# Attention of a hybrid decoder layer: a written order on four engines in place of a scheduled one, and row minima in place of row maxima

## The chip, the core and the metric

One core of a Trainium2 chip runs the whole layer in one launch. The metric is the device time of that launch in microseconds (us). The engines named below work side by side, each through its own queue in order: TensorE (PE, with its weight loads shown as PEld), VectorE (DVE), ScalarE (ACT), GpSimd (POOL) and SyncE (SP), which issues the transfers from memory. One waits for another only where a semaphore makes it.

## What is computed

A decoder layer on 512 positions of width 1024, in float32: RMS norm, one input projection, eight attention heads of 64 beside a gated linear recurrence, an output projection, then a gated feed-forward part. The change touches the attention heads alone. With 512 positions in blocks of 256 and three blocks to choose, every earlier block is chosen, so the attention is plain causal attention with a bias by distance:

```python
scale = HEAD_DIM ** -0.5
...
s_own = jnp.einsum("bhqd,bhkd->bhqk", qc, k_own) * scale
s_own = s_own + bias_T[head, t5_bucket(q_pos - k_pos)]
s_own = jnp.where(q_pos >= k_pos, s_own, -jnp.inf)
...
p = jax.nn.softmax(logits, axis=-1)
out = jnp.einsum("bhqk,bhkd->bhqd", p, v)
...
mix = jnp.concatenate([attn, lru], axis=-1) @ w_out
```

## The kernel before

Products are made from split operands. A float32 tile is cast to an upper half by ACT (`split`, line 84) and the rest, the lower half, is made by DVE (line 85); a product is then three matmuls (`mm3`, lines 79 to 81). Weights are split the same way: one 128x1024 cast on ACT (`wh`) and one subtraction of the same size on DVE (`wl`).

Attention goes by pairs of heads (`pr`, four of them, 128 rows of q and k each), in a pair by heads (`s`, two) and in a head by blocks of 128 queries (`i`, four). A tile (`pr`, `s`, `i`) covers the 128(i+1) keys up to its queries. Its steps, with the names that the trace uses:

- `psc`, two matmuls (lines 636 and 637): scores, first with the upper half of the keys (`sk`), then with the lower half (`klz`);
- `st`: line 640 on DVE adds the bias (`tb`) and takes the row's maximum, line 643 scales that maximum by a constant, line 644 on ACT takes the exponential and its sum, lines 646 and 647 on DVE take the reciprocal and scale the row;
- `ptp`, one transpose for each block of 128 keys (line 653), split into `pTh` (ACT) and `pTl` (DVE);
- after a head's last tile `pav`, eight matmuls with the values (line 663), drained by ACT and DVE into `pair` (lines 666, 667). After a pair's second head `pair` is split into `mixT`, the left operand of the output projection.

A pair's q and k come from `pq`: 16 pieces of three matmuls each, 48 matmuls in all; `pq` is then cast and subtracted into `sq`, `sk` and `klz` (lines 623 to 627). There is one `klz` tile for all pairs. PSUM banks are three for `pq` (shared later with `py`), two for `psc`, two for `ptp` and one for `pav`.

Up to line 578 the order on PE, ACT, DVE and SP is the order in which the code is written (`manual_schedule`, closed by `written.close()`). From there on a scheduler decides, by its own model of the engines, which ready instruction each queue gets next. The code of the attention only gives it a first order: `softmax` of a tile comes three tiles (`LAG`) ahead of its transposes, and three pieces (`FILL`) of the next pair's projection follow each tile. The scheduler fills PE with matmuls of the output projection (`py`) once the projections `pq` are used up.

Of the kernel before, what the change touches and what calls it, by code (L numbers as in the profile page):

```python
# [18 lines left out]
P = 128  # L19
S = 512  # L20
# [19 lines left out]
ISCALE = DH ** -0.5  # L40
FE = S + P
EW = 3 * P
FILL = 3
LAG = 3
assert MAX_DISTANCE <= P

# [6 lines left out]
def hybrid_layer(  # L53
# [16 lines left out]
    def bank(name, tag):  # L70
        return ps.tile([P, 512], F32, tag=tag, name=name, bufs=BANKS[tag])
# [26 lines left out]
    def at(hl, *idx):  # L98
        return hl[0][idx], hl[1][idx]
# [469 lines left out]
    for t in range(NT):  # L569
        pg = bank("pgr", "mm")  # L570
        for k in range(KD):
            mm3(pg, at(w_gr[t], slice(None), k), at(hT, slice(None), k), k == 0, k == KD - 1)
        if t >= 2:
            first_w.append(split_w(first_qk[:, :, t - 2], KD, P))
# [17 lines left out]
    heads = {}  # L592
# [5 lines left out]
    def head_pair(pr):  # L598

        tb = ap_.tile([P, 2, S], F32, tag="tb", name="tb")  # L600
# [6 lines left out]
        if pr:  # L607
            raw = load_qk(pr)
        ws = [split_w(raw[:, :, i], KD, P) for i in range(2)] if pr else first_w
        yield  # L610

        proj = []
        for w in ws:
            pq = bank("pq", "mm")
            for k in range(KD):
                mm3(pq, at(w, slice(None), k), at(hT, slice(None), k), k == 0, k == KD - 1)
                yield
            proj.append(pq)
        qs, ks = (ap_.tile([P, 2, S], F32R, tag=f"s{i}", name=f"s{i}") for i in "qk")
        kl = klz  # L620
        for s in range(2):
            me, other = own[s], own[1 - s]
            nc.scalar.copy(qs[me, s], proj[0][me])
            nc.vector.tensor_sub(qs[other, s], proj[0][me], f32(qs[me, s]))
            nc.scalar.copy(ks[me, s], proj[1][me])
            nc.scalar.copy(ks[other, s], proj[1][me])
            nc.vector.tensor_sub(kl[me, s], proj[1][me], f32(ks[me, s]))
        heads[pr] = qs, ks, kl, tb

    def softmax(pr, s, i):  # L630

        qs, ks, kl, tb = heads[pr]
        W = P * (i + 1)
        psc = bank("psc", "sc")
        qi = slice(i * P, (i + 1) * P)
        nc.tensor.matmul(psc[:, :W], qs[:, s, qi], ks[:, s, :W], start=True, stop=False)
        nc.tensor.matmul(psc[:, :W], qs[:, s, qi], kl[:, s, :W], start=False, stop=True)
        st = ap_.tile([P, S], F32, tag="st", name="st", bufs=4)
        sm = ap_.tile([P, 4], F32, tag="sm", name="sm", bufs=4)
# [7 lines left out]
        nc.vector.tensor_scalar(st[:, :W], st[:, :W], sm[:, 3:4], None, op0=ALU.mult)  # L647
        return st

    def transposed(st, pT, i):  # L650
        ptr = bank("ptp", "tr")
        for j in range(i + 1):
            nc.tensor.transpose(ptr[:, j * P:(j + 1) * P], st[:, j * P:(j + 1) * P], ident)  # L653
        split(by_keys(pT[0], i), by_keys(pT[1], i),
              ptr[:, :P * (i + 1)].rearrange("p (j q) -> p j q", q=P))

    def attend(pr, s, pT, pair):
        me, other = own[s], own[1 - s]
        pav = bank("pav", "av")
        for j in range(NT):  # L660
            vs = vhl[:, j, pr, 2 * s:2 * s + 2].rearrange("p a d -> p (a d)")
            for i in range(2):
                nc.tensor.matmul(  # L663
                    pav[:, j * P:], vs, pT[i][:, j * S:j * (S - P) + S],
                    start=j == 0 and i == 0, stop=j == NT - 1 and i == 1)
        nc.scalar.copy(pair[me], pav[other])
        nc.vector.tensor_add(pair[me], pav[me], pair[me])
        if s == 1:
            split(mixT[0][:, pr], mixT[1][:, pr], pair)

    tiles = [(pr, s, i) for pr in range(NPAIR) for s in range(2) for i in range(NT)]
    for _ in head_pair(0):
        pass
    ahead, sts, last = iter(()), [], None
    for n in range(-LAG, len(tiles)):
        if 0 <= n + LAG < len(tiles):
            pr, s, i = tiles[n + LAG]
            if s == 0 and i == 0:  # L680
                for _ in ahead:
                    pass
                if pr + 1 < NPAIR:
                    ahead = head_pair(pr + 1)
                    next(ahead)
            sts.append(softmax(pr, s, i))
        for _ in itertools.islice(ahead, FILL):
            pass
        if n < 0:
            continue  # L690
        pr, s, i = tiles[n]
        if i == 0:
            if last:
                attend(*last)
            if s == 0:
                pair = ap_.tile([P, S], F32, tag="pair", name="pair", bufs=1)
            pT = [ap_.tile([P, 3 * (S - P) + S], F32R, tag=f"pT{j}", name=f"pT{j}", bufs=1)
                  for j in "hl"]
            last = pr, s, pT, pair
        transposed(sts.pop(0), pT, i)  # L700
    attend(*last)

    attn_stack.close()

# [194 lines left out]
```

## Time and profile before

| | us |
|---|---|
| median of 3 runs | 585.26 (585.23 to 585.57) |
| the profiled execution | 586.3 |
| its span, first to last instruction | 584.2 |
| PE busy | 572.6 (98%) |
| PE weight loads busy | 473.5 (81%) |
| DVE busy | 360.3 (62%) |
| ACT busy | 279.7 (48%) |
| mean granted TensorE clock | 0.997 of full speed |

The profiled execution stands 2.1 us above its span and 1.0 us above the median of the timed runs. Shares of busy time are means over stages with different limits. A matmul's duration is longer than its distance to the next one, since matmuls are pipelined: its cost is read from one start to the next. The same holds for DVE and ACT, whose instructions overlap a little.

### The profile page before, as it was taken

The numbers are of one execution on the slowest core, as the hardware profiler recorded it, in microseconds if no ns is written. First come the engines' busy times: TensorE is split into PE (matmuls) and PEld (weight loads), VectorE is DVE, ScalarE is ACT, GpSimd is POOL, SyncE is SP. The second block draws the span as 40 slices with busy tenths as digits, with TensorE's granted clock in tenths as the row PEclk, the third lists the DMA queues.
The fourth block names the chain that finished last, engine by engine and source line by source line (L and its number), as shares of the span: only waits on it lengthen the run. The fifth ranks groups of instructions, "written<-read, shape, count | busy, mean of one in ns | idle before, by whom it ended". The sixth has DMA issues, their size and how long they took to land.

```text
span 584.2 us, 7051 instructions
## 1 busy us (share of the span) xinstructions
PE 572.6 (98%) x2734; PEld 473.5 (81%) x2734; DVE 360.3 (62%) x649; ACT 279.7 (48%) x457; POOL 15.9 (3%) x37
## 2 busy tenths in 40 slices
PE   8999999999999999999999999999999999999995
PEld 4988888787788889888888888888888888888884
DVE  5787777889896895656656656656656522241225
ACT  6568856778775663543444444344344322132121
POOL 2150000000000000000000000000000000000000
PEclk9999999999999999999999999999999999999998
DMA  9533626333202614012412422422424223332103
GB/s 269 157 109 115 212 72 193 98 107 108 73 1 70 217 44 139 1 55 90 145 63 82 144 70 76 145 72 73 144 73 144 73 72 107 100 119 73 37 0 144
DMA packets 53449, 59.62 MB, mean 102 GB/s; under 512 B 2480, under 2 KB 42624, under 8 KB 53417
## 3 DMA queue, kind: packets, MB, share of 16 engines
q1 hardware_dynamic: 53319, 59.11, 31.7%
q8 instruction: 21, 0.34, 0.3%
q10 hardware_dynamic: 98, 0.07, 0.1%
q14 instruction: 11, 0.09, 0.1%
HBM read 57.06 MB, written 3.69 MB: 104 GB/s over the span
## 4 chain that ended last, share of the span: by engine, by line
PE 91%; DVE 4%; ACT 3%; DMA 1%; issue 1%; DVEq 0%; SPq 0%; ACTq 0%
PE pup L80 14%; PE pup L81 14%; PE pup L79 14%; PE py L81 8%; PE py L80 8%; PE py L79 8%; PE px L309 3%; PE pq L79 2%; PE pq L80 2%; PE pq L81 2%; PE pav L663 2%; PE ptp L653 1%; PE pgr L80 1%; PE pgr L79 1%; PE pv L80 1%; PE pv L79 1%
## 5 line engine op out<-in xcount | busy, mean ns | idle before, releaser
L85 DVE TENSOR_TENSOR wl<-raw,wh 128x1024 fp32r<-128x1024 f32 x78 | 95.3, 1222 | 125.6 <-ACT wh L84 125.3
L84 ACT CAST wh<-raw 128x1024 fp32r<-128x1024 f32 x78 | 81.8, 1050 | 139.9 <-PE py L81 72.2
L81 PE MATMUL pup<-h2Th,wl 128*128 128x512 f32 x320 | 124.5, 389 | 0.0
L80 PE MATMUL pup<-h2Tl,wh 128*128 128x512 f32 x320 | 124.5, 389 | 0.0
L79 PE MATMUL pup<-h2Th,wh 128*128 128x512 f32 x320 | 124.3, 389 | 0.0
L80 PEld LDWEIGHTS pup<-h2Tl,wh 128*128 128x128 f32 x320 | 60.1, 188 | 12.5
L79 PEld LDWEIGHTS pup<-h2Th,wh 128*128 128x128 f32 x320 | 60.0, 188 | 12.5
L81 PEld LDWEIGHTS pup<-h2Th,wl 128*128 128x128 f32 x320 | 60.1, 188 | 12.3
L79 PE MATMUL py<-wh,acth 128*128 128x512 f32 x176 | 68.9, 391 | 0.0
L81 PE MATMUL py<-wh,actl 128*128 128x512 f32 x176 | 68.8, 391 | 0.0
L80 PE MATMUL py<-wl,acth 128*128 128x512 f32 x176 | 68.8, 391 | 0.0
L79 PEld LDWEIGHTS py<-wh,acth 128*128 128x128 f32 x176 | 33.1, 188 | 7.2
L81 PEld LDWEIGHTS py<-wh,actl 128*128 128x128 f32 x176 | 33.1, 188 | 7.2
L80 PEld LDWEIGHTS py<-wl,acth 128*128 128x128 f32 x176 | 33.1, 188 | 7.2
L821 DVE SCALAR_TENSOR_TENSOR yu<-pup,par,yu 128x511 f32<-128x511 f32 (+1 forms) x44 | 33.0, 749 | 4.3 <-ACT yu L819 3.5
L828 ACT ACTIVATE yg<-yg 128x512 f32<-128x512 f32 x22 | 14.0, 635 | 44.7 <-DVE yg L821 44.7
L821 DVE SCALAR_TENSOR_TENSOR yg<-pup,par,yg 128x511 f32<-128x511 f32 (+1 forms) x44 | 32.8, 747 | 2.0 <-ACT yg L819 1.2
L829 DVE TENSOR_TENSOR yu<-yu,yg 128x512 f32<-128x512 f32 x22 | 15.2, 693 | 18.0 <-ACT yg L828 18.0
L81 PE MATMUL py<-wh,mixTl 128*128 128x512 f32 x64 | 25.4, 397 | 0.0
L79 PE MATMUL pq<-hTh,wh 128*128 128x512 f32 x64 | 25.4, 397 | 0.0
L81 PE MATMUL pq<-hTh,wl 128*128 128x512 f32 x64 | 25.3, 395 | 0.0
L79 PE MATMUL py<-wh,mixTh 128*128 128x512 f32 x64 | 25.3, 395 | 0.0
(213 smaller groups left out, 939.6 us busy)
## 6 DMA issues: line engine op xcount, KB each, us to landing
raw<-in_w_up_dram SPq DMA_DIRECT2D x22, 1024.0 KB, 5.1
raw<-in_w_down_dram SPq DMA_DIRECT2D x10, 1024.0 KB, 5.5
raw<-in_w_in_dram SPq DMA_DIRECT2D x4, 1024.0 KB, 5.1
rawqk<-in_w_in_dram SPq DMA_DIRECT2D x8, 512.0 KB, 5.2
raw<-in_w_out_dram SPq DMA_DIRECT2D x4, 1024.0 KB, 5.6
raw<-in_w_in_dram SPq DMA_DIRECT2D x4, 512.0 KB, 9.1
out_dram<-yz SPq DMA_DIRECT2D x8, 256.0 KB, 2.0
xres<-in_x_dram SPq DMA_DIRECT2D x3, 512.0 KB, 6.2
```

The lines of the kernel that those rows point to most:

```text
L79: nc.tensor.matmul(o, lh, rh, start=start, stop=False)
L80: nc.tensor.matmul(o, lh, rl, start=False, stop=False)
L81: nc.tensor.matmul(o, ll, rh, start=False, stop=stop)
L84: nc.scalar.copy(h, src)
L85: (sub or nc.vector).tensor_sub(l, src, f32(h))
L309: nc.tensor.matmul(p_x[t][:, cs], w_x[t][i == LH][:, k], hT[i == HL][:, k, cs], start=first and n == 0, stop=last and n == len(todo) - 1)
L653: nc.tensor.transpose(ptr[:, j * P:(j + 1) * P], st[:, j * P:(j + 1) * P], ident)
L663: nc.tensor.matmul(pav[:, j * P:], vs, pT[i][:, j * S:j * (S - P) + S], start=j == 0 and i == 0, stop=j == NT - 1 and i == 1)
L821: nc.vector.scalar_tensor_tensor(y[:, d:], pt[:, :S - d], w_conv_f(2 - d, blk), y[:, d:], op0=ALU.mult, op1=ALU.add)
L828: nc.scalar.activation(yg, yg, AF.Gelu_apprx_tanh)
L829: nc.vector.tensor_mul(yu, yu, yg)
```

## The change

The change writes the attention's order out by hand. `written.close()` moves from before the attention to the tile `n == 8 * (NPAIR - 2) + 4`, the first tile of the third pair's second head (counted in transposes); from there on the scheduler decides again, as it also may place instructions that come later in the code between written ones on ACT and DVE.

The generator `head_pair` becomes functions for each step, and a loop over `n` from -3 calls them in a fixed order. In a turn of the loop, tile `n` is transposed, tile `m = n + 3` gets its scores, tile `m - 1` its quotients, tile `n` its halves, tile `m` its extreme value and exponential. `PIECES` says how many pieces of `pq` a turn gets, and a list by `o = n % 8` says in which turn a pair's casts, weight splits, drains and bias loads stand. The raw weights of pairs 0 and 1 are loaded together ahead of the recurrence's end. The argument `nc.vector` of `w_split` names the engine that `split_w` takes anyway.

Scores are scaled by -1/8 and the bias is subtracted in sign (`scale=-ISCALE`, `op1=ALU.min`), so that the row's minimum is already the exponential's bias: line 643, one small DVE instruction for each of 32 tiles, goes away.

```diff
-    first_qk = load_qk(0)
+    raw_qk = {0: load_qk(0), 1: load_qk(1)}
...
-    written.close()
...
+    def cast_k(pr, s):
+        ks = qk_tiles(pr)[1]
+        me, other = own[s], own[1 - s]
+        nc.scalar.copy(ks[me, s], p_qk[pr, 1][me])
+        nc.scalar.copy(ks[other, s], p_qk[pr, 1][me])
+        nc.vector.tensor_sub(klz[me, s], p_qk[pr, 1][me], f32(ks[me, s]))
...
         nc.vector.tensor_tensor_reduce(
-            out=st[:, :W], in0=psc[:, :W], in1=tb[:, s, S - W:S], scale=1.0, scalar=NEG,
-            op0=ALU.add, op1=ALU.max, accum_out=sm[:, 0:1])
-        nc.vector.tensor_scalar(sm[:, 1:2], sm[:, 0:1], -ISCALE, None, op0=ALU.mult)
-        nc.scalar.activation(st[:, :W], st[:, :W], AF.Exp, scale=ISCALE, bias=sm[:, 1:2],
-                             accum_out=sm[:, 2:3])
+            out=sts[m][:, :W], in0=psc[m][:, :W], in1=tbs[pr][:, s, S - W:S], scale=-ISCALE,
+            scalar=-NEG, op0=ALU.add, op1=ALU.min, accum_out=sms[m][:, 0:1])
+
+    def exponentials(m):
+        st, sm = sts[m][:, :P * (tiles[m][2] + 1)], sms[m]
+        nc.scalar.activation(st, st, AF.Exp, scale=-1.0, bias=sm[:, 0:1], accum_out=sm[:, 2:3])
...
+    PIECES = {5: 3, 6: 3, 7: 2, 0: 1, 1: 3, 2: 2, 3: 2, 4: 0}
+    bias(0)
+    bias(1)
+    raw_qk[2] = load_qk(2)
+    pieces(0, KD)
+    w_split(1, 0)
+    cast_q(0, 0)
+    w_split(1, 1)
+    raw_qk[3] = load_qk(3)
+    pieces(0, KD)
+    cast_k(0, 0)
+    pieces(1, 3)
+    late = None
     for n in range(-LAG, len(tiles)):
...
+        pr, o, m = n // 8, n % 8, n + LAG
+        if n >= 0:
+            turned(n)
+        if m < len(tiles):
+            scores(m)
+        if 0 <= m - 1 < len(tiles):
+            quotients(m - 1)
+        if n >= 0:
+            if late is not None:
+                turned_halves(late)
+                late = None
+            if n > 0 and n % NT == 0:
+                late = n
+            else:
+                turned_halves(n)
+
+        nxt = pr + 2 if o >= 5 else pr + 1
+        if nxt < NPAIR:
+            pieces(nxt, PIECES[o] - (n < 0))
+        if n > 0 and n % NT == 0:
+            values(*tiles[n - 1][:2])
+        if m < len(tiles):
+            maxima(m)
+        if o == 0:
+            if pr + 1 < NPAIR:
+                cast_q(pr + 1, 0)
+            if pr + 2 < NPAIR:
+                w_split(pr + 2, 0, nc.vector)
+        elif o == 1 and pr > 0:
+            drain(pr - 1, 1)
+        elif o == 2 and pr > 0:
+            mix(pr - 1)
+        elif o == 3 and pr + 2 < NPAIR:
+            w_split(pr + 2, 1, nc.vector)
+        elif o == 4 and pr + 1 < NPAIR:
+            cast_k(pr + 1, 0)
+        elif o == 5 and pr >= 0:
+            drain(pr, 0)
+            if pr + 2 < NPAIR:
+                bias(pr + 2)
+        elif o == 6 and pr + 1 < NPAIR:
+            cast_k(pr + 1, 1)
+        elif o == 7 and pr + 1 < NPAIR:
+            cast_q(pr + 1, 1)
+        if m < len(tiles):
+            exponentials(m)
+        if n == 8 * (NPAIR - 2) + 4:
+            written.close()
+    values(NPAIR - 1, 1)
+    drain(NPAIR - 1, 1)
+    mix(NPAIR - 1)
```

Where the third pair's scores begin, PE's queue before the change had this (`psc` 128 wide is the new pair's first tile; the two `psc` with `klz` above it belong to the pair that ends):

```order
L663 MATMUL pav<-pTh,vhl 128x256
L637 MATMUL psc<-klz,sq 128x384
L637 MATMUL psc<-klz,sq 128x512
L663 MATMUL pav<-pTl,vhl 128x256
L663 MATMUL pav<-pTh,vhl 128x128
L663 MATMUL pav<-pTl,vhl 128x128
L636 MATMUL psc<-sk,sq 128x128
L637 MATMUL psc<-klz,sq 128x128
L653 MATMUL ptp<-ident,st 128x128 x2
```

In the changed kernel (its lines 669, 644, 645 and 686 are the transposes, the two score matmuls and the values) the same place reads:

```order
L686 MATMUL pav<-pTh,vhl 128x128
L686 MATMUL pav<-pTl,vhl 128x128
L669 MATMUL ptp<-ident,st 128x128 x2
L644 MATMUL psc<-sk,sq 128x128
L645 MATMUL psc<-klz,sq 128x128
L78 MATMUL pq<-hTh,wh 128x512
L79 MATMUL pq<-hTl,wh 128x512
L80 MATMUL pq<-hTh,wl 128x512
```

Each score product's two matmuls and each head's eight value matmuls now stand together, the transposes come ahead of the scores, and all of the next pair's pieces stand behind the second score matmul.

DVE's queue before, for the same pair's `klz` (line 627; `wl` from `raw` is a weight of the output projection):

```order
L640 ISA sm 128x1
L643 TENSOR_SCALAR sm<-sm 128x1
L85 TENSOR_TENSOR wl<-raw,wh 128x1024
L646 RECIPROCAL sm<-sm 128x1
L647 TENSOR_SCALAR st<-st,sm 128x256
L627 TENSOR_TENSOR klz<-pq,sk 64x512
L85 TENSOR_TENSOR pTl<-ptp,pTh 128x3x128
L85 TENSOR_TENSOR pTl<-ptp,pTh 128x4x128
L627 TENSOR_TENSOR klz<-pq,sk 64x512
L640 ISA st,sm<-psc,tb 128x384
```

And in the changed kernel, from tile 11's lower half (line 84) to the `klz` (line 635) of the third pair's first head; line 652 is the biased minimum, lines 663 and 664 the quotients:

```order
L84 TENSOR_TENSOR pTl<-ptp,pTh 128x4x128
L652 ISA st,sm<-psc,tb 128x384
L652 ISA sm 128x1
L84 TENSOR_TENSOR wl<-rawqk,wh 128x1024
L84 TENSOR_TENSOR wl<-raw,wh 128x1024
L663 RECIPROCAL sm<-sm 128x1
L664 TENSOR_SCALAR st<-st,sm 128x384
L652 ISA st,sm<-psc,tb 128x512
L652 ISA sm 128x1
L635 TENSOR_TENSOR klz<-pq,sk 64x512
L84 TENSOR_TENSOR wl<-raw,wh 128x1024
```

`klz` moved from ahead of the old pair's last two lower halves of 3 and 4 blocks to behind them and behind two weight splits, one quotient and one more minimum.

## Rows read from the trace of the kernel before

**Rows 1.** The page, busy time of each engine.

```profile
PE 572.6 (98%) x2734; PEld 473.5 (81%) x2734; DVE 360.3 (62%) x649; ACT 279.7 (48%) x457; POOL 15.9 (3%) x37
```

**Rows 2.** Stretches: length, then busy PE, PEld, DVE, ACT, POOL; clock, DMA share, GB/s.

```profile
101.90:119.90 18.00, 17.71 (x87) 14.23 (x87) 14.41 (x46) 12.98 (x28) 0.00 (x0) 1.00 0.45 142
119.90:139.50 19.60, 19.16 (x100) 15.58 (x100) 17.75 (x58) 15.04 (x36) 0.00 (x0) 1.00 0.25 80
159.10:178.80 19.70, 19.63 (x110) 16.12 (x111) 16.54 (x64) 13.46 (x37) 0.00 (x0) 1.00 0.01 4
```

**Rows 3.** Timeline of PE (start us, us long, what), first and last of 57 projections.

```profile
88.79 0.39 PE L79 MATMUL pq<-hTh,wh 128*128 128x512 f32 x1
...
101.48 0.39 PE L81 MATMUL pq<-hTh,wl 128*128 128x512 f32 x1
```

**Rows 4.** Timeline of PE where its starts stand apart.

```profile
101.94 0.50 PE L636 MATMUL psc<-sk,sq 128*128 128x128 f32 x2
...
116.32 0.39 PE L81 MATMUL pq<-hTh,wl 128*128 128x512 f32 x1
116.83 0.50 PE L663 MATMUL pav<-pTh,vhl 128*128 128x512 f32 x1
117.16 0.40 PE L79 MATMUL pq<-hTh,wh 128*128 128x512 f32 x1
...
119.43 0.22 PE L663 MATMUL pav<-pTh,vhl 128*128 128x128 f32 x1
119.49 0.27 PE L663 MATMUL pav<-pTl,vhl 128*128 128x128 f32 x1
119.91 0.33 PE L636 MATMUL psc<-sk,sq 128*128 128x128 f32 x1
...
132.68 0.49 PE L653 MATMUL ptp<-ident,st 128*128 128x128 f32 x3
132.93 0.42 PE L636 MATMUL psc<-sk,sq 128*128 128x384 f32 x1
133.67 0.66 PE L653 MATMUL ptp<-ident,st 128*128 128x128 f32 x4 [0.32 <-DVE pTl L85]
```

**Rows 5.** Waits of 101 to 182 us: total us, times, longest us.

```profile
PEld ptp L653 <- DVE pTl L85: 1.5, 3, 0.6
PEld pav L663 <- ACT pTh L84: 1.5, 5, 0.5
```

**Rows 6.** Timeline of DVE in the second pair.

```profile
125.89 0.69 DVE L640 CUSTOM_DVE_ANT_0 st<-psc,tb 128x512 f32<-128x512 f32 x1
...
126.50 0.16 DVE L646 RECIPROCAL sm<-sm 128x1 f32<-128x1 f32 x1
126.58 1.21 DVE L85 TENSOR_TENSOR wl<-raw,wh 128x1024 fp32r<-128x1024 f32 x1
127.70 0.42 DVE L647 TENSOR_SCALAR st<-st,sm 128x384 f32<-128x384 f32 x1
128.03 0.69 DVE L85 TENSOR_TENSOR pTl<-ptp,pTh 128x512 fp32r<-128x512 f32 x1
128.63 0.15 DVE L643 TENSOR_SCALAR sm<-sm 128x1 f32<-128x1 f32 x1
128.69 0.28 DVE L640 CUSTOM_DVE_ANT_0 st<-psc,tb 128x128 f32<-128x128 f32 x1
...
135.21 0.16 DVE L646 RECIPROCAL sm<-sm 128x1 f32<-128x1 f32 x1
135.40 0.35 DVE L647 TENSOR_SCALAR st<-st,sm 128x256 f32<-128x256 f32 x1
135.67 0.68 DVE L627 TENSOR_TENSOR klz<-pq,sk 64x512 fp32r<-64x512 f32 x1
```

**Rows 7.** Timeline of ACT in the second pair.

```profile
126.33 0.57 ACT L84 CAST pTh<-ptp 128x512 fp32r<-128x512 f32 x1
...
128.87 0.73 ACT L644 ACTIVATE st<-st,sm 128x512 f32<-128x512 f32 x1 [1.36 <-DVE sm L643]
```

More of the change, by code (lines that the diff above doesn't have):

```diff
@@ L42 @@
 EW = 3 * P
-FILL = 3
 LAG = 3
@@ L591, in hybrid_layer @@
     own = (slice(0, DH), slice(DH, P))
-    heads = {}
     klz = ap_.tile([P, 2, S], F32R, name="klz", bufs=1)
@@ L606, in head_pair @@
             ap=[[EW - 1, P], [P * EW, 2], [1, 2 * P]]))
[L607 to L632, printed above, removed]
+    def w_split(pr, i, eng=None):
+        w_qk[pr, i] = split_w(raw_qk[pr][:, :, i], KD, P, eng)
@@ new lines, in pieces, with qk_tiles @@
+    def pieces(pr, count):
+        for n in range(n_done.get(pr, 0), n_done.get(pr, 0) + count):
+            i, k = divmod(n, KD)
+            if k == 0:
+                p_qk[pr, i] = bank("pq", "mm")
+            mm3(p_qk[pr, i], at(w_qk[pr, i], slice(None), k), at(hT, slice(None), k),
+                k == 0, k == KD - 1)
+        n_done[pr] = n_done.get(pr, 0) + count
+    def qk_tiles(pr):
+        if pr not in qkt:
+            qkt[pr] = [ap_.tile([P, 2, S], F32R, tag=f"s{i}", name=f"s{i}") for i in "qk"]
+        return qkt[pr]
@@ new lines, in cast_q, with scores @@
+    def cast_q(pr, s):
+        qs = qk_tiles(pr)[0]
+        me, other = own[s], own[1 - s]
+        nc.scalar.copy(qs[me, s], p_qk[pr, 0][me])
+        nc.vector.tensor_sub(qs[other, s], p_qk[pr, 0][me], f32(qs[me, s]))
+    def cast_k(pr, s):
+        ks = qk_tiles(pr)[1]
+        me, other = own[s], own[1 - s]
+        nc.scalar.copy(ks[me, s], p_qk[pr, 1][me])
+        nc.scalar.copy(ks[other, s], p_qk[pr, 1][me])
+        nc.vector.tensor_sub(klz[me, s], p_qk[pr, 1][me], f32(ks[me, s]))
+    def scores(m):
+        pr, s, i = tiles[m]
@@ L633, in softmax @@
         W = P * (i + 1)
-        psc = bank("psc", "sc")
+        qs, ks = qkt[pr]
+        psc[m] = bank("psc", "sc")
         qi = slice(i * P, (i + 1) * P)
[L636 to L639, printed above, removed]
-        nc.vector.tensor_tensor_reduce(
-            out=st[:, :W], in0=psc[:, :W], in1=tb[:, s, S - W:S], scale=1.0, scalar=NEG,
-            op0=ALU.add, op1=ALU.max, accum_out=sm[:, 0:1])
@@ L643, in softmax @@
-        nc.vector.tensor_scalar(sm[:, 1:2], sm[:, 0:1], -ISCALE, None, op0=ALU.mult)
-        nc.scalar.activation(st[:, :W], st[:, :W], AF.Exp, scale=ISCALE, bias=sm[:, 1:2],
-                             accum_out=sm[:, 2:3])
-        nc.vector.reciprocal(sm[:, 3:4], sm[:, 2:3])
[L647 to L653, printed above, removed]
+        nc.tensor.matmul(psc[m][:, :W], qs[:, s, qi], ks[:, s, :W], start=True, stop=False)
@@ new lines, in scores, with maxima @@
+        nc.tensor.matmul(psc[m][:, :W], qs[:, s, qi], klz[:, s, :W], start=False, stop=True)
+    def maxima(m):
+        pr, s, i = tiles[m]
+        W = P * (i + 1)
+        sts[m] = ap_.tile([P, S], F32, tag="st", name="st", bufs=4)
+        sms[m] = ap_.tile([P, 4], F32, tag="sm", name="sm", bufs=4)
+        nc.vector.tensor_tensor_reduce(
+            out=sts[m][:, :W], in0=psc[m][:, :W], in1=tbs[pr][:, s, S - W:S], scale=-ISCALE,
+            scalar=-NEG, op0=ALU.add, op1=ALU.min, accum_out=sms[m][:, 0:1])
@@ new lines, in exponentials, with quotients, turned @@
+    def exponentials(m):
+        st, sm = sts[m][:, :P * (tiles[m][2] + 1)], sms[m]
+        nc.scalar.activation(st, st, AF.Exp, scale=-1.0, bias=sm[:, 0:1], accum_out=sm[:, 2:3])
+    def quotients(m):
+        st, sm = sts[m][:, :P * (tiles[m][2] + 1)], sms[m]
+        nc.vector.reciprocal(sm[:, 3:4], sm[:, 2:3])
+        nc.vector.tensor_scalar(st, st, sm[:, 3:4], None, op0=ALU.mult)
+    def turned(n):
+        ptp[n] = bank("ptp", "tr")
+        for j in range(tiles[n][2] + 1):
+            nc.tensor.transpose(
+                ptp[n][:, j * P:(j + 1) * P], sts[n][:, j * P:(j + 1) * P], ident)
@@ L654, in transposed, with turned_halves @@
+    def turned_halves(n):
+        pr, s, i = tiles[n]
+        if i == 0:
+            pTs[pr, s] = [ap_.tile([P, 3 * (S - P) + S], F32R, tag=f"pT{j}", name=f"pT{j}", bufs=1)
+                          for j in "hl"]
+        pT = pTs[pr, s]
         split(by_keys(pT[0], i), by_keys(pT[1], i),
[L655 to L659, printed above, removed]
+              ptp[n][:, :P * (i + 1)].rearrange("p (j q) -> p j q", q=P))
@@ L660, in attend, with values @@
+    def values(pr, s):
+        pav[pr, s] = bank("pav", "av")
         for j in range(NT):
@@ L663, in attend @@
                 nc.tensor.matmul(
-                    pav[:, j * P:], vs, pT[i][:, j * S:j * (S - P) + S],
+                    pav[pr, s][:, j * P:], vs, pTs[pr, s][i][:, j * S:j * (S - P) + S],
                     start=j == 0 and i == 0, stop=j == NT - 1 and i == 1)
[L666 to L669, printed above, removed]
-    tiles = [(pr, s, i) for pr in range(NPAIR) for s in range(2) for i in range(NT)]
@@ L674, in hybrid_layer @@
-    for _ in head_pair(0):
-        pass
-    ahead, sts, last = iter(()), [], None
-    for n in range(-LAG, len(tiles)):
[L678 to L700, printed above, removed]
@@ L701, in hybrid_layer, with drain, mix @@
-    attend(*last)
+    def drain(pr, s):
+        me, other = own[s], own[1 - s]
+        if s == 0:
+            pairs[pr] = ap_.tile([P, S], F32, tag="pair", name="pair", bufs=1)
+        pair = pairs[pr]
+        nc.scalar.copy(pair[me], pav[pr, s][other])
+        nc.vector.tensor_add(pair[me], pav[pr, s][me], pair[me])
+    def mix(pr):
+        split(mixT[0][:, pr], mixT[1][:, pr], pairs[pr])
+    tiles = [(pr, s, i) for pr in range(NPAIR) for s in range(2) for i in range(NT)]
+    psc, sts, sms, ptp, pTs, pav, pairs = {}, {}, {}, {}, {}, {}, {}
```

7 lines of the change are left out of this document (4 added, 3 removed).

## The prediction

> **What bounds the kernel now.** I read the page's busy times first. PE is busy for 98% of the span [rows 1], and the change adds no matmul and takes none away, so it can only alter the time in which PE does not move at its own pace. Next the stretches of the attention [rows 2]: PE is again nearly always busy, and DVE stands right behind it, with 17.75 of 19.60 us in the second pair of heads (the third reads the same to the hundredth). ACT has 4.6 us to spare there. So there is one engine that ends the stage, and a second one with under a tenth of slack.
>
> Busy PE hides short waits, so I then went through PE's timeline by distances from start to start. Projection matmuls follow each other every 0.227 us (57 of them start from 88.79 to 101.48, 56 distances) [rows 3]; a 128-wide one takes 0.06 (119.43 to 119.49), and a transpose 0.11 (three in 0.49, of which the last takes some 0.27) [rows 4]. Distances above that are waits [rows 4]: before the first scores 0.46 in place of 0.23; before the first values 0.51 in place of 0.23; before a pair's first scores 0.42 in place of 0.06, three times in three pairs; behind the 384-wide scores 0.74 in place of 0.18, twice; a first value matmul that stands alone takes 0.33 in place of 0.23, five times. That makes 0.23 + 0.28 + 1.1 + 1.1 + 0.5 = 3.2 us. The whole is a little more. From 101.94 to the fourth pair's first scores at 159.1 are 57.2 us, in which PE starts 148 wide matmuls (135 `pq`, 13 `py`; 33.5 us), 51 transposes (5.6), the scores of 24 tiles (2560 columns for a head, 1.13 us, and some 0.25 for the narrow ones whose weight load shows: six times 1.38, 8.3) and five heads of values (1.16 each, 5.8): 53.2 us. **About 4.0 us are waits**, the most the new order can win there. The view of waits names the lower and upper halves `pTl` and `pTh` as what PE waits for [rows 5].
>
> **The change part by part.** *Minima.* Line 643 goes away, 32 times. It costs DVE 0.06 us (128.63 to 128.69) [rows 6], 1.9 us over the attention, and the exponential may start that much sooner. PE sees none of it directly.
>
> *Quotients.* In the new order each reciprocal is followed at once by the scaling that needs it. The rows show 0.19 us from such a reciprocal to its scaling (135.21 to 135.40), and 0.08 where another instruction follows (126.50 to 126.58) [rows 6]. For the 24 written tiles that is up to 24 x 0.11 = 2.6 us more on DVE, less what was adjacent before. So DVE's work stays where it was. The Trainium skill (VectorE: DVE Perf Modes, section The DRAIN you can't avoid) says that the next instruction starts only when the pipe has emptied, whether or not a semaphore stands between. By that rule adjacency would cost nothing, and the sum below would be some 0.2 us lower; the two rows differ by 0.11 us, and I go by them.
>
> *The argument `nc.vector`* names the engine that was taken anyway: nothing. *Loads.* On SP the first two bias loads now stand ahead of the third and fourth pair's weights, and the fourth pair's bias stands behind a load of the output projection that waits for a weight split in turn 11. All are used many turns later, and DMA's share is 0.45 and below [rows 2]: nothing. If that cover failed, one landing of a bias tile would come on top; I keep it out.
>
> *PE's order.* What was split up (scores, values) stands together, so the 0.5 us of lone value matmuls go. The waits at the first scores go as well: 57 projections stand ahead of them as before, but ACT no longer has a further weight cast in front of `sk`. What comes late instead is read from the written order, by walking one turn of the loop after another with the durations above.
>
> Take turn 11 (the tile with four transposes, near the end of the second pair). PE needs from its start to the second score matmul of tile 16, the third pair's first: 4 transposes 0.44, scores 0.35, two pieces 1.36; one transpose 0.11, scores 0.46, values 1.16; two transposes 0.22, first score matmul 0.14: 4.24 us. That matmul needs `klz`, which DVE makes at the end of this chain: transposes done 0.66 [rows 4], cast of four blocks 0.57 [rows 7], lower half 0.60, minimum over 384 about 0.48 (between 0.61 at 512 and 0.2 at 128), two weight splits of 1.12, reciprocal and scaling 0.19 + 0.33, minimum over 512 0.61, `klz` 0.68 [rows 6], and some 0.05 for each of three changes of engine: 6.5 us. **PE waits 2.3 us**, and the nine projections behind it cannot pass. This holds however punctual DVE was before. The same place one pair earlier (turns 3 to 5) has one weight split in the chain: 5.4 against 4.24, **1.2 us**.
>
> A second, smaller one: in turns 8 and 16 a piece of `pq` takes the bank that the last `sq` of turn 7 or 15 sets free. Chain 0.66 + 0.57 + 0.60 + 0.48 + 0.69 + 0.15 = 3.15, PE 0.44 + 0.35 + 1.36 + 0.11 + 0.46 = 2.72: 0.4 us each; in turn 0 about 0.2. New waits at least: 1.2 + 2.3 + 0.8 + 0.2 = 4.5 us.
>
> At most: in the first turns PE has little to do (turns -3 to 0 hold 5.6 us of it), while each DVE step waits for an exponential (0.73 at 512 and the read of its sum behind it [rows 7]) of the step before. Walked from there, DVE reaches turn 4 late enough that the first head's values wait 0.3 and turn 5 waits 0.7 more: 5.5 us. A check by load: eight turns hold 18.2 us of PE (16 pieces 10.9, 20 transposes 2.2, scores 2.8, values 2.3). DVE's 17.75 held two weight splits; turns 8 to 15 hold five, and lose eight scalings: 17.75 + 3 x 1.12 - 0.5 = 20.6. DVE is 2.4 us longer than PE there, about what the waits of turns 8 and 13 make together.
>
> *Sum.* Waits removed 4.0, added 4.5 to 5.5: +0.5 to +1.5 us; in the part that the scheduler still orders (19.7 us, DVE busy 16.54 [rows 2]) I see no sign either way and allow 0.5. I take +0.9. Made against the profiled execution, 586.3 + 0.9 = 587.2 us; that execution stands 1.0 above the median of the timed runs, so 586.2 us for the time asked.
>
> **The rivals.** *Waits traded for waits* (the forecast): 585.2 to 587.4. *The order keeps PE fed.* The waits that [rows 5] names all end, and `klz` comes in time because some step of my chain is overlapped (ACT's cast of the second weight, DVE's start of it). Then 4.0 go and the bank waits of 0.8 come: 582.1. For it: those waits are bubbles of one turn, which is what an order by hand removes. Against it: the chain stands in DVE's queue row by row, with nothing in it that can be skipped.
>
> *DVE takes over as the bound* (the slower side). Place: turns 8 to 21. With five weight splits in eight turns DVE falls behind, has too little room to recover by turn 21, and the last stretch begins with the softmax late; the six `py` that the scheduler put there (1.4 us) don't cover it. Price: the upper 1.5 and some 1.0 in the last stretch, 587.8. It decides once DVE is busy over 95% from turn 8 to 21. For it: the 20.6 us; against it: turns 16 to 20 hold one split only. The Trainium skill (Perfetto Trace Analysis, section Optimization Strategy) advises to interleave stretches whose most-contended engines differ; this order gathers weight splits where DVE is already short, and [rows 2] agree that DVE had a tenth to spare.
>
> *Nothing moves*: the waits change names one for one, 585.3.
>
> **How the numbers follow.** About 0.2% (1.2 us) is what a measurement of this kernel can tell from no change. The forecast has 0.55, of which 0.37 lie within 0.2% and 0.18 above; fed PE 0.18, faster; DVE as bound 0.21, slower; nothing moves 0.06. So faster 0.18, same 0.43, slower 0.39. The forecast's own range is 585.2 to 587.4; with the upper case whole, and the lower one cut where two in ten are left out, 583.6 to 588.2.
>
> **What would show it.** In the profile after: PE's start-to-start distance before the second score matmul of tiles 8 and 16 near 1.2 to 1.9 and 2.3 us, released by `klz` from DVE; 0.4 before the first projection of turns 8 and 16, released by `sq`; no lone value matmuls; DVE busy over 95% from turn 8 to 13; the eight turns of the second pair near 20.9 us in place of 19.6. Wrong if `klz` lands before PE reaches it, or if the distance of tiles 8 to 24 shrinks below 39 us.

## The result, and the profile after

The changed kernel takes 591.25 us (median of four runs: 589.74, 589.86, 592.64, 593.45) against 585.41 us before, a ratio of 1.0097 (95% interval 1.0079 to 1.0114). The forecast was 586.2, at most 588.2. The two faster runs had a mean granted clock of 0.998, the two slower ones 0.996 and 0.993. The profiled execution took 592.64 us with a span of 590.5, 6.3 longer than before.

The page's busy times:

```profile
PE 575.2 (97%) x2734; PEld 475.1 (80%) x2734; DVE 360.0 (61%) x617; ACT 277.2 (47%) x457; POOL 16.2 (3%) x37
```

The stretches of [rows 2], with the third pair's between them (columns as there):

```profile
101.90:119.90 18.00, 16.23 (x82) 12.81 (x81) 14.41 (x42) 12.85 (x31) 0.00 (x0) 1.00 0.47 115
119.90:139.50 19.60, 18.52 (x99) 15.22 (x97) 17.69 (x48) 15.02 (x34) 0.00 (x0) 1.00 0.22 75
139.50:159.10 19.60, 18.06 (x87) 14.90 (x88) 16.62 (x45) 13.21 (x32) 0.00 (x0) 0.91 0.39 133
159.10:178.80 19.70, 18.29 (x100) 14.01 (x99) 18.05 (x59) 15.37 (x40) 0.00 (x0) 1.00 0.17 54
```

PE is busy 1.5, 0.6 and 1.3 us less than in [rows 2], DVE as long in the first two and 1.5 us longer in the last, the scheduler's part. In the third pair the clock is 0.91, where the kernel before had 1.00 in all four.

PE's timeline shows the two places that the prediction named, in turns 5 and 13, and what stands behind the second:

```profile
117.23 0.40 PE L669 MATMUL ptp<-ident,st 128*128 128x128 f32 x2
118.46 0.33 PE L644 MATMUL psc<-sk,sq 128*128 128x128 f32 x1 [0.83 <-ACT sk L634]
119.47 0.33 PE L645 MATMUL psc<-klz,sq 128*128 128x128 f32 x1 [0.68 <-DVE klz L635]
...
137.76 0.41 PE L669 MATMUL ptp<-ident,st 128*128 128x128 f32 x2
139.16 0.33 PE L644 MATMUL psc<-sk,sq 128*128 128x128 f32 x1 [0.99 <-ACT sk L634]
140.80 0.33 PE L645 MATMUL psc<-klz,sq 128*128 128x128 f32 x1 [1.31 <-DVE klz L635]
140.96 0.45 PE L78 MATMUL pq<-hTh,wh 128*128 128x512 f32 x1
...
142.30 0.63 PE L80 MATMUL pq<-hTh,wl 128*128 128x512 f32 x1
142.73 0.63 PE L78 MATMUL pq<-hTh,wh 128*128 128x512 f32 x1
143.15 0.63 PE L79 MATMUL pq<-hTl,wh 128*128 128x512 f32 x1
...
145.46 0.40 PE L79 MATMUL pq<-hTl,wh 128*128 128x512 f32 x1
145.69 0.39 PE L80 MATMUL pq<-hTh,wl 128*128 128x512 f32 x1
```

From 117.23 to 119.47 two transposes and one narrow matmul need 0.3 us (at [rows 4]' pace): 1.9 us of wait, in two halves, the first released by `sk` from ACT and the second by `klz` from DVE. In turn 13 it is 2.7, again in two such halves. From 141.9 to 145.3 the starts of `pq` stand 0.43 apart in place of 0.23: the granted clock is at its lower level, 1.2 GHz, for 3.4 us that begin 1.1 us behind the end of the long wait.

**A ledger.** For the comparisons below I added up, over PE's timeline from the attention on, each distance from start to start less the pace of that matmul (0.227 us for 512 columns, 0.175 for 384, 0.119 for 256, 0.06 for 128, 0.109 for a transpose). The sum is PE's lost time, waits and lower clock alike; each row is one profiled execution. A turn reaches from one tile's transposes to the next's; S, Q and C are three edits (of the weight split, the quotients and the casts) told with the experiments, whose numbers stand in brackets.

| us lost in | start to turn 4 | 5, 6 | 7 to 12 | 13, 14 | 15 to 20 | 21 to 31 | behind |
|---|---|---|---|---|---|---|---|
| before | 2.3 | 0.5 | 2.1 | 0.5 | 2.1 | 2.0 | 3.3 |
| after | 1.8 | 2.3 | 1.2 | 4.7 | 1.7 | 4.3 | 2.5 |
| S (2) | 1.8 | 2.1 | 2.2 | 1.8 | 2.3 | 3.8 | 3.3 |
| Q (9) | 1.4 | 4.3 | 0.9 | 5.1 | 1.1 | 3.7 | 2.4 |
| C (13) | 1.7 | 3.6 | 1.6 | 5.0 | 2.2 | 3.6 | 2.1 |
| S, Q (11) | 1.4 | 2.1 | 1.4 | 1.8 | 2.9 | 3.2 | 3.5 |
| C, S (14) | 1.8 | 1.2 | 2.6 | 1.3 | 2.3 | 3.8 | 3.3 |
| C, S, Q (12) | 1.4 | 0.5 | 1.7 | 0.4 | 2.9 | 3.4 | 3.4 |
| the same, maxima (16) | 2.3 | 0.6 | 2.8 | 0.6 | 5.3 | 2.8 | 3.3 |

After against before: +5.7 us. Of turn 13's and 14's 4.7, the slow stretch is 1.6 (the excess of its distances, 141.93 to 145.46). The 0.6 that is missing to the spans' 6.3 lies ahead of the attention: its first projection starts at 89.37 against [rows 3]' 88.79, and over the profiles whose code is the same up to there it starts between 87.6 and 89.4.

Rows with and without the lower clock are not alike: Q and C have a slow stretch at both places (turns 5 and 13, 6 and 14), and 16 has one in turn 17, each worth 1.6 us by the same excess; S and the combinations of S, Q and C have none. With 1.6 taken off for each stretch the rows add up to 12.8 before and 16.9 after, 17.3 for S, 15.7 for Q, 16.6 for C, 16.3 for either pair, 13.7 for all three and 16.1 with maxima.

### The profile page after: what moved, and what is told of

It is laid out like the page before. It is cut to its first block, busy times and chain, and to the rows that moved or that the text cites. A ratio compares the mean times of both kernels' runs of the same rounds, so it can differ in the third digit from the quotient of the medians.

```text
span 590.5 us, 7028 instructions
## 1 busy us (share of the span) xinstructions
PE 575.2 (97%) x2734; PEld 475.1 (80%) x2734; DVE 360.0 (61%) x617; ACT 277.2 (47%) x457; POOL 16.2 (3%) x37
## 4 chain that ended last, share of the span: by engine, by line
PE 86%; DVE 6%; DMA 3%; ACT 2%; issue 1%; SPq 0%; DVEq 0%; ACTq 0%
PE pup L79 14%; PE pup L78 14%; PE pup L80 14%; PE py L80 8%; PE py L78 8%; PE py L79 8%; PE px L308 3%; PE pq L78 2%; DMA raw<-in_w_up_dram 2%; PE pq L79 2%; PE pq L80 2%; DVE wl L84 2%; PE ptr L159 1%; PE pgr L79 1%; PE pv L79 1%
## 5 line engine op out<-in xcount | busy, mean ns | idle before, releaser
L79 PE MATMUL pq<-hTl,wh 128*128 128x512 f32 x64 | 25.4, 397 | 0.0
```

Of the source, the lines that this page charges most:

```text
L79: nc.tensor.matmul(o, lh, rl, start=False, stop=False)
```

## The experiments

Ratios are against the kernel before on the same chip, each kernel ran four to twelve times. Line numbers are the changed kernel's.

**1. Work in the wait of tile 16**

```diff
+        for _ in range(8 if m == 16 else 0):
+            nc.tensor.matmul(psc[m], hT[0][:, 0, :P], hT[0][:, 0], start=True, stop=True)
         nc.tensor.matmul(psc[m][:, :W], qs[:, s, qi], ks[:, s, :W], start=True, stop=False)
```

> Eight extra 512-column matmuls (hTh by hTh into the score bank, overwritten by the real product) stand ahead of tile 16's first score matmul, where TensorE waits 2.3 us in the changed kernel. They add work and remove none; the order elsewhere is the same. Clock theory (the pq matmuls behind this wait are 0.43 us apart for some 3.3 us because TensorE stood still, and that is part of the loss): the extra matmuls (8 x 0.227 = 1.8 us) lie in the wait, the pq matmuls of 141.9 to 145.2 are 0.227 apart again, no slice below 9 in PEclk there, and the time falls by about 2 us against the changed kernel's 591.3, to 589.3; the runs should also scatter less. Rival (the slow stretch has nothing to do with the wait, or the wait alone is the loss): the time stays at 591.3 or rises by up to 1.8 us, and the 0.43 us distances stay.

591.05 us (1.0101, interval 1.0084 to 1.0117); four runs lie at 590.9 to 591.2, one at 593.45. In the profile the slow stretch is gone:

```profile
139.50:159.10 19.60, 19.02 (x100) 15.28 (x99) 18.15 (x49) 14.53 (x34) 0.00 (x0) 1.00 0.31 103
```

The ledger of turns 13 and 14, with the 1.8 us of extra matmuls counted as lost, is 3.1 in place of 4.7: the clock theory holds for the stretch in this profile. The time does not follow, since in this profile PE waits 2.0 us for a transposed row block at 208 us, behind a load of `w_up`, where the kernel after lost 0.4. So the lower clock costs some 1.6 us where it comes; that this gain reaches the end is not shown. The changed kernel's own two runs at a mean clock of 0.998 (589.74 and 589.86) are below every run of this experiment.

**2. The second weight split later (S), and 3. with the casts first in turn 4**

```diff
-        elif o == 3 and pr + 2 < NPAIR:
-            w_split(pr + 2, 1, nc.vector)
...
         elif o == 6 and pr + 1 < NPAIR:
             cast_k(pr + 1, 1)
+            if pr + 2 < NPAIR and pr >= 0:
+                w_split(pr + 2, 1, nc.vector)
```

In 3, `cast_k(pr + 1, 0)` also moves ahead of the quotients of turn `o == 4`.

> The second weight split of a pair moves from turn 3 (11) to turn 6 (14); with it the first two splits of w_out leave turns 11 and 12. Wait theory (the loss is TensorE waiting for sk and klz at tiles 8 and 16, plus the half clock behind the second): tile 8's wait falls from 1.5 to 0.4 us (one 1.22 us lower half and one 0.6 us cast less ahead), tile 16's from 2.3 to near 0.3 (two lower halves, 2.35 us, less ahead), the 0.43 us distances go (2.0): -1.1 -2.0 -2.0, so 586.2 against 591.3. Rival (DVE is the bound in turns 8 to 21): the same DVE work in the same stretch only stands elsewhere; the waits turn up at other transposes or score matmuls and the time stays within 1 us of 591.3.

> The weight split moved as in the run before, and cast_k of the next pair's first head put first in turns 4 and 12, ahead of the quotients, maxima and exponential. Wait theory: both waits (tile 8 and tile 16, 1.5 and 2.3 us) go to near zero and the half clock with them: 591.3 - 1.5 - 2.3 - 2.0 = 585.5, with the scheduler's part +-0.5; quotients and maxima of turn 4 stand 0.68 us later, which may cost up to 0.7 us each time. Rival (DVE the bound): 590 to 591, the waits move to ptp<-st.

591.09 (1.0090) and 592.41 (1.0115): nothing gained. In 2 the loss at tile 16 falls by 2.9 us, of which 1.6 are the slow stretch that this profile doesn't have, but tile 8 loses nearly as much as ever: its `sk` stands on ACT behind the exponential of tile 6, which waits for a minimum (ACT's timeline of 2):

```profile
114.81 0.62 ACT L659 ACTIVATE st<-st,sm 128x384 f32<-128x384 f32 x1 [1.29 <-DVE sm L652]
...
115.42 0.56 ACT L633 CAST sk<-pq 64x512 fp32r<-64x512 f32 x1
```

In 3, 2.1 us of the waits at the score matmuls stay, and 3.4 come at transposes (`ptp` on `pTl`). The wait theory, in its simple form, does not hold.

**4. Minima alone, in the kernel before**

```diff
-            out=st[:, :W], in0=psc[:, :W], in1=tb[:, s, S - W:S], scale=1.0, scalar=NEG,
-            op0=ALU.add, op1=ALU.max, accum_out=sm[:, 0:1])
-        nc.vector.tensor_scalar(sm[:, 1:2], sm[:, 0:1], -ISCALE, None, op0=ALU.mult)
+            out=st[:, :W], in0=psc[:, :W], in1=tb[:, s, S - W:S], scale=-ISCALE, scalar=-NEG,
+            op0=ALU.add, op1=ALU.min, accum_out=sm[:, 0:1])
```

> The kernel before with nothing but the minima: scale and sign turned in the reduction, the 32 small multiplications of L643 gone, exp with scale -1; the scheduler still orders the attention. By my prediction's step, 32 x 0.06 = 1.9 us of DVE work goes, of which at most the waits of TensorE on DVE chains (about 1 of the 4.0 us) are on the path: 584.4 to 585.4. Rival (the scheduler orders the attention otherwise when a small instruction is gone, and that order decides): anything from 583 to 589, with other rows of PE in this stretch.

585.98 (1.0003, 0.9994 to 1.0011): nothing. "PE sees none of it directly" was right for the scheduler's order.

**5. Scores of tiles 8 and 16 behind nine projections.** In turns `o == 5`, `scores(m)` moves behind `pieces(...)`.

> On TensorE alone, in turns 5 and 13 (and -3) the score matmuls of the new pair's first tile stand behind the turn's nine projection matmuls (9 x 0.227 = 2.04 us) instead of ahead of them. The two waits, 2.0 us at tile 8 and 2.8 us at tile 16, are then covered for 2.0 us each, and with TensorE busy there is no half clock behind the second. Wait theory: -2.0 -2.0 and, in the runs that had it, -2.0 more of half clock: 586 to 587 against 591.3 (589.7 in the better runs of the changed kernel). Rival (VectorE and ScalarE run behind by a turn anyway and only their chain counts): the wait turns up at the next transposes, and the time stays above 589.

590.28 (1.0075, 1.0061 to 1.0090). The wait moves to the next transposes, as the rival said (PE's timeline):

```profile
119.60 0.27 PE L645 MATMUL psc<-klz,sq 128*128 128x128 f32 x1
120.70 0.55 PE L669 MATMUL ptp<-ident,st 128*128 128x128 f32 x3 [0.82 <-DVE pTl L84]
...
141.86 0.55 PE L669 MATMUL ptp<-ident,st 128*128 128x128 f32 x3 [1.60 <-DVE pTl L84]
```

**6. The scheduler orders the new code, and 7. orders it from turn 13 on.** `written.close()` stands ahead of the attention, or behind `n == 12`.

> The changed kernel's code with the written order ended where the kernel before ends it, ahead of the attention: minima, lower halves on VectorE, loads and the new loop stay, and the scheduler orders the attention. Theory (the order is the whole loss): 585 to 587, the two long waits gone. Rival (other parts of the change, the lower halves on VectorE or the loads, take part of it): 588 to 591.

> The written order ends behind turn 12 instead of turn 20, so tile 8 (turn 5) still has its place by the written order and tile 16 (turn 13) is ordered by the scheduler. Wait theory: tile 8's 2.0 us stay, tile 16's 2.8 us go to 0.5 or less as in the kernel before, and with them the half clock (2.0): 591.3 - 2.3 - 2.0 = 587.0, and the last stretch as in the kernel before, if its 2.6 us come from the later place of the w_out splits: not below 586. Rival (the loss is in the last stretch, turns 21 to 31, whoever orders turn 13): 590 or more.

589.01 (1.0049, 1.0034 to 1.0065) and 589.02 (1.0045). So ending the written order early gives back 2.2 us by the medians and 2.8 by the ratios, of 5.8, and the way in which the code is now written costs the rest even when the scheduler orders it; what in it does so is not settled. By the same ledger 6 loses some 3.9 us in turns 21 to 31, about as much as after (4.3) and more than before (2.0). In 7 turns 13 and 14 lose some 1.3 in place of 4.7, and the lower clock came behind tile 8 instead, whose wait is the same 1.9 us as after (distances of 0.43 from 119.09 to 122.08):

```profile
117.00:122.00 5.00, 3.69 (x10) 2.91 (x11) 3.99 (x13) 2.89 (x8) 0.00 (x0) 0.71 0.83 258
```

**8. Maxima and L643 back, in the written order**

> The changed kernel with maxima in place of minima again: the small multiplication stands once more between each maximum and its exponential, 32 x 0.06 us of VectorE and some 0.2 us of latency on each chain. My prediction's step (minima save up to 1.9 us of VectorE, of which what lies in the waits counts): in the written order each of the two long waits has two of them in its chain, so +0.2 to +1.0: 591.5 to 592.3. Rival (nothing on the path): 591.0 to 591.4.

596.98 (1.0191, 1.0172 to 1.0210): +5.7 us for an instruction that costs nothing in the kernel before. Both theories had far less. Its profile has slow stretches at both places, one more than after, so 1.6 us of the difference between the two profiles are the lower clock.

That asked for another theory. The view of waits from 101 to 160 us (total, times, longest), first of the kernel after, then of before, and DVE's timeline after:

```profile
ACT st L659 <- DVE sm L652: 12.0, 13, 2.1
```

```profile
ACT st L644 <- DVE sm L643: 4.3, 5, 1.4
```

```profile
114.10 0.08 DVE L652 DVE_READ_ACCUMULATOR2_ANT sm<- 128x1 f32 x1
114.91 0.16 DVE L663 RECIPROCAL sm<-sm 128x1 f32<-128x1 f32 x1 [0.73 <-ACT st L659]
115.11 0.35 DVE L664 TENSOR_SCALAR st<-st,sm 128x256 f32<-128x256 f32 x1
115.38 0.69 DVE L84 TENSOR_TENSOR pTl<-ptp,pTh 128x512 fp32r<-128x512 f32 x1
115.99 0.55 DVE L652 CUSTOM_DVE_ANT_0 st<-psc,tb 128x384 f32<-128x384 f32 x1
```

ACT stands 12.0 us for minima, and DVE stands for each exponential: with the quotient of tile m - 1 written ahead of the minimum of tile m, the two engines go round one ring a turn (minimum, exponential, reciprocal, quotient, lower half, next minimum), and on this reading neither can catch up. I called this the ring.

**9 to 12. The quotients out of the ring (Q), then with maxima, with S, and with S and the casts in turn 3 (C)**

```diff
-        if 0 <= m - 1 < len(tiles):
-            quotients(m - 1)
...
         if m < len(tiles):
             maxima(m)
+        if 0 <= m - 1 < len(tiles):
+            quotients(m - 1)
...
+        elif o == 3 and pr + 1 < NPAIR:
+            cast_k(pr + 1, 0)
-        elif o == 4 and pr + 1 < NPAIR:
-            cast_k(pr + 1, 0)
```

> One line moves: in each turn the quotients of the tile before stand behind this turn's minimum on VectorE, not ahead of the lower half and the minimum. Ring theory (in the written order VectorE and ScalarE run in one ring of a turn each: minimum, exponential, reciprocal, quotient, lower half, next minimum, so VectorE stands for each exponential, 0.6 to 0.7 us a turn, and ScalarE 12.0 us in 101 to 160 us for minima; whatever is put in the ring makes the turn longer): the exponential drops out of the ring, ScalarE's 12.0 us fall below 8, the casts of tiles 8 and 16 come earlier by 0.5 to 1.3 us each, and the time falls by 2 to 4 us (with the half clock behind the waits gone or not): 587.3 to 589.3. Rival (only the two chains ahead of tiles 8 and 16 count, and the weight splits in them): within 0.8 us of 591.3.

> As the run before (quotients behind the minimum), with maxima and the small multiplication in place of minima. With the quotients in their written place the multiplication cost 5.7 us (597.0 against 591.3). Ring theory: out of the ring it costs its 32 x 0.06 to 0.1 us at most where VectorE is full: +0.5 to +2.0 on the run before. Rival (the multiplication costs through VectorE's busy time wherever it stands): again +4 to +6.

> Quotients behind the minimum, and the second weight split in turn 6 (14) instead of 3 (11). In the written ring the moved split gave nothing (591.1), since the waits came again in turns 9 and 17. Ring theory: with the exponential out of the ring, the split's 1.2 us (2.35 at tile 16) now come off the waits of tiles 8 and 16 and are not asked back: 1.5 to 3 us below the run of the quotients alone, 585 to 587. Rival (VectorE is full): within 0.8 us of that run.

> As the run before, and cast_k of the next pair's first head in turn 3 (11), right behind the projection that it reads, ahead of that turn's exponential. Ring theory: sk and klz are there before tiles 8 and 16 are scored, both waits below 0.3 us, no half clock, waits of TensorE in 101 to 160 us no more than the kernel before's 5.4: 584 to 586, level with the kernel before. Rival (the last stretch by the scheduler, 160 to 182 us, keeps its 2.6 us whatever stands ahead): 587 to 588.

Q alone: 591.79 (1.0116), runs from 588.41 at a mean clock of 0.999 to 596.16 at 0.987. ACT's wait at the exponentials falls from 12.0 to 7.2 us, in two lines of the view of waits:

```profile
ACT st L659 <- DVE sm L663: 4.3, 5, 1.8
ACT st L659 <- DVE sm L652: 2.9, 6, 1.1
```

The first line names the reciprocal that now starts together with the minimum's last row; those exponentials start 0.10 us behind that row's end, as in the kernel after (112.27 to 112.36), so I count both lines as waits for minima. The ledger still shows 4.3 and 5.1 us lost at the same two places, 1.6 of each by the lower clock. That clock hides a gain: without it Q's ledger is 1.2 us below the kernel after's, and its one run at 0.999 is 1.4 us below that kernel's best two. With maxima 596.85: again +5.1, so leaving the ring does not take the multiplication's price away. The ring alone is not the cause either. S and Q: 588.96 (1.0063). **All three: 586.25 (1.0014, 1.0005 to 1.0022)**, turns 5, 6, 13 and 14 back at the kernel before's loss. ACT still waits 8.8 us for minima there (6.2 and 2.6 in the same two lines), so that wait by itself does not set the time.

**13, 14. Which of the three**

> Of the last version's three edits the casts alone: cast_k of the next pair's first head in turn 3 (11), ahead of the weight split, which stays there; quotients in their written place. If the place of these casts is the cause (TensorE meets the score matmuls of tiles 8 and 16 before sk and klz are cast): both waits fall below 0.5 us, the half clock goes, and the time is 587 or less against 591.3. If the split and the quotients carry the gain, it stays at 589 to 591, with the wait at the transposes of turns 6 and 14.

> Casts in turn 3 (11) and the second weight split in turn 6 (14); quotients in their written place, ahead of the minimum. Beside the version with all three edits (586.25) this shows what the ring of minimum, exponential and quotient is worth once no long wait is left. Ring theory: +1 to +3, 587.3 to 589.3, with VectorE standing 0.6 to 0.7 us a turn for the exponential. Rival (the ring has slack as soon as the casts are early): within 0.5 us of 586.25.

C alone 592.50 (1.0106), C and S 589.29 (1.0060). Alone, C ends the waits at the score matmuls, and about the same time is lost at the next transposes, again with the lower clock behind (waits of PE from 101 to 160 us, of 13):

```profile
PE ptp L669 <- DVE pTl L84: 5.3, 3, 3.2
```

Without C 2.7 us of the gain are missing and without Q 3.0; Q and C without S were not tried. No single one gives anything in the medians.

**15, 16. The split in turn 4, and maxima in the best version**

> All three edits, with the second split in turn 4 (12), where VectorE has least to do (a minimum of 512 columns and one quotient, 1.25 us, in a turn of 2.2 us on TensorE), instead of turn 6 (14). If VectorE's load turn by turn sets the waits that are left (0.7 to 1.2 us in turns 9, 16 and 17), it gains 0.3 to 1 us on 586.25, level with the kernel before or below it; if those waits come from the other split in turns 0 and 8, nothing.

> The version with all three edits, with maxima and the small multiplication in place of minima. In the changed kernel the multiplication cost 5.7 us, in the kernel before (minima alone) 0.0. If its price there came from lengthening the chains ahead of tiles 8 and 16 and the half clock behind them, it costs here, where those waits are gone, 0 to 1.5 us: 586.3 to 587.8. If VectorE's busy time is the bound in this stretch whatever the order, it costs 3 to 5 us again: 589 to 591.

15: 586.60 (1.0010, 1.0001 to 1.0018), level with 12; the kernel before isn't beaten. 16: 590.86 (1.0085), +4.6 on 12; in the ledger +4.0, of which 1.6 are the lower clock in turn 17, behind a wait of 2.1 us. DVE's timeline of 16 and of 12 at the same place:

```profile
113.17 0.08 DVE L652 DVE_READ_ACCUMULATOR2_ANT sm<- 128x1 f32 x1
113.29 0.15 DVE L655 TENSOR_SCALAR sm<-sm 128x1 f32<-128x1 f32 x1
113.36 0.15 DVE L664 RECIPROCAL sm<-sm 128x1 f32<-128x1 f32 x1
```

```profile
112.22 0.08 DVE L652 DVE_READ_ACCUMULATOR2_ANT sm<- 128x1 f32 x1
112.22 0.16 DVE L663 RECIPROCAL sm<-sm 128x1 f32<-128x1 f32 x1
```

Directly behind the row that it reads, the multiplication takes 0.19 us of DVE, not the 0.06 of [rows 6], where the scheduler had put another instruction between. In 16 it stands so in 21 of the first 24 tiles: 4.0 us of DVE. In the ledger 2.4 us of that are waits of PE and 1.6 the lower clock behind them, though the waits of turns 5 and 13 are gone: in this order DVE has little slack.

**17, 18. The weight splits of turns 0 to 11 on GpSimd, in the changed kernel and in 15** (`nc.gpsimd` for `nc.vector` in both `w_split` calls)

> The changed kernel with the four weight splits of turns 0 to 11 on GpSimd instead of VectorE (GpSimd's 128x1024 lower half took 2.4 us in the prologue, VectorE's 1.22); nothing else moves. Full-VectorE theory (in the written order VectorE is the last in turns 4 to 17, and each 0.1 us on it is 0.1 us of the time, as the 24 multiplications of 0.19 us were 4.6 us): 4 x 1.1 us leave it, of which the one in turn 0 stands ahead of a stretch with slack, so -2.5 to -4.5: 587 to 589 against 591.3. Rival (only the wait for sk and klz on ScalarE counts): the casts of the upper halves stay on ScalarE, -0.5 to -1.5: 590 to 591. Third: the lower half, twice as long on GpSimd, is late for the projections or slows VectorE: 591 or more.

> The version with the casts in turn 3, the split in turn 4 and the quotients behind the minimum (586.6), with its four weight splits on GpSimd. Full-VectorE theory: the waits left in turns 9, 16 and 17 (0.2, 1.0 and 1.0 us above the pace) lose most of what VectorE causes, -1 to -2: 584.6 to 585.6, level with or below the kernel before's 585.9. Rival (what is left comes from the last stretch and the order of the scheduler): 586 to 587.

597.23 (1.0173) and 588.25 (1.0030, 1.0015 to 1.0045, against 1.0001 to 1.0018 for 15): 17 is 6.0 us slower than the kernel after, half of it by the lower clock, which this profile has for 10.2 us in place of 3.4; 18 is no faster than 15. GpSimd's and DVE's timelines of 17:

```profile
108.66 2.40 POOL L84 TENSOR_TENSOR wl<-rawqk,wh 128x1024 fp32r<-128x1024 f32 x1 [13.57 <-ACT wh L83]
115.99 2.37 POOL L84 TENSOR_TENSOR wl<-rawqk,wh 128x1024 fp32r<-128x1024 f32 x1 [4.93 <-ACT wh L83]
```

```profile
108.42 0.68 DVE L628 TENSOR_TENSOR sq<-pq,sq 64x512 fp32r<-64x512 f32 x1
...
109.48 1.87 DVE L664 TENSOR_SCALAR st<-st,sm 128x512 f32<-128x512 f32 x1
...
117.20 1.38 DVE L664 TENSOR_SCALAR st<-st,sm 128x384 f32<-128x384 f32 x1
...
120.32 0.49 DVE L664 TENSOR_SCALAR st<-st,sm 128x512 f32<-128x512 f32 x1
```

A quotient that meets GpSimd's split takes 1.87 us in place of 0.49 and ends just behind it. For each split moved DVE is rid of 1.2 us, and the quotients that meet the two splits shown take 1.4 and 1.0 us longer: the test took little work off DVE, and does not settle the theory that DVE is full.

## Why the prediction missed

*What held.* No matmul was added; the waits ahead of the second score matmuls of tiles 8 and 16 came, 1.9 and 2.7 us for "1.2 to 1.9" and "2.3"; DVE was full from turn 8 into 13; the lone value matmuls went. The second pair's eight turns (126.54 to 149.49) took 22.95 us, 21.35 without the slow stretch, for "20.9". Two signs came out otherwise. `klz` ended each wait but released only half of it: PE first stood 0.8 and 1.0 us for `sk`, ACT's upper half, for which the prediction's chain had no step. And the waits of 0.4 at the projections of turns 8 and 16 did not come.

*The step that failed is the sum, "+0.5 to +1.5 ... I take +0.9"*, in three of its terms, by the ledger:

- *"Waits removed 4.0"* is too large. Turns 5, 6, 13 and 14 lose 4.4 us more than before without the clock, about what the forecast added there (1.2 + 2.3, and 0.7 more at most in turn 5). That count is already net of the 1.0 that these turns lost before, so 3.0 of the 4.0 should have gone elsewhere; only 1.8 did (2.8 in all), as turns 9 and 17 lose 0.4 and 0.5 anew. Up to turn 20 that makes +2.6.
- *The last stretch*, allowed "0.5", is +2.3 in turns 21 to 31, and +1.5 with what is won behind them.
- *The lower clock*, 1.6 us in this profile, stood in no term.

The three make the ledger's +5.7.

*What stood behind it.* I priced waits one at a time. Experiments 2, 3, 5, 9 and 13 took away one wait or one cause each, and the median fell by at most 1.0 us (1.3 by the ratios); the loss came again at a later instruction of DVE's and ACT's written queues, or as lower clock. All three edits together gave 5.0, in the ledger 3.2 of waits and 1.6 of lower clock. So the written places of split, quotients and casts are shown to carry that part together. That the ring joins them is argued, not shown.

"DVE takes over as the bound" was the nearest rival, with too small a price, but it is borne out in part only. Its condition, over 95% from turn 8 to 21, held into turn 13 (16.39 of 17.00 us, below) and not behind it (16.62 of 19.60 from 139.5 to 159.1, above). Its 1.0 in the last stretch was 1.5 to 2.3, and DVE is busy 18.05 us there in place of 16.54; but 6, where nothing stands in a written order, loses 3.9 in turns 21 to 31 and 12 still 3.4. That late work of DVE is the cause there is therefore not shown.

```profile
126.50:143.50 17.00, 14.63 (x74) 11.93 (x73) 16.39 (x42) 13.12 (x29) 0.00 (x0) 0.96 0.26 86
```

*Minima* were priced by a row of a schedule that mostly had something to put in the gap: 0.06 and nothing on the path there, 0.19 here. With maxima the change would have cost 11 us (596.98). *Quotients:* the rows' 0.11 us of adjacency was the right side: in the kernel after, the scaling starts 0.20 us behind its reciprocal (114.91 to 115.11). The Trainium skill (VectorE: DVE Perf Modes, section The DRAIN you can't avoid) measured that a semaphore after each of eight copies costs nothing extra. The trace does not agree for these small dependent instructions: 0.12 us from the start of a minimum's last row to that of the multiplication which reads it in 16, against 0.00 to an independent reciprocal in 12.

*Open.* Why the new code under the scheduler (589.0) is 3.3 us behind the old by the medians (2.9 by the ratio); why turns 21 to 31 lose more in every version of the new code than before; why the lower clock comes in some executions and not in others; what is left in turns 15 to 31 of version 12 (6.3 us lost against 4.1).

## What to carry to other kernels

Where two engines are within a tenth of full, price an order by hand turn by turn on every engine, and not as single waits: look for an instruction that waits for the other engine ahead of one that could run. One edit that gains nothing is no proof that its place is harmless; try the edits together before dropping them. Compare two profiles only after their stretches of lower clock are taken out. Price an instruction at the place where it will stand: directly behind its operand the multiplication cost three times what it did in a gap.

## What was not expected of the hardware

- Behind waits of TensorE of 1.9 us and more the clock fell to 1.2 GHz for about 3.4 us, in some executions: the 1.9 us at tile 8 brought it in 7 and not in the kernel after. One such stretch cost 1.6 us, and version 9 has runs from 588.4 (mean clock 0.999) to 596.2 us (0.987). The Trainium skill (TensorE: Matmul & The Clock Gate, section HAM oscillation) tells of matmuls at half rate behind each wait for a transfer; the trace agrees on the half rate, here with waits for other engines and not behind each.
- GpSimd's subtraction stops DVE's scaling from SBUF to SBUF until it ends (1.87 for 0.49 us), while the subtraction that reads PSUM beside it (108.42) took its usual 0.68. The Trainium skill (SBUF — State Buffer, section Who interferes with whom) calls it an exclusive port pair, taken for a whole instruction by the engine that starts first; the trace agrees: the subtraction started at 108.66, the scaling behind it at 109.48.
